# Splitting q and k into high and low parts for two attention heads in one 128-row operation, with transfers within SBUF placing each head's rows

## The chip, the cores and the metric

The kernel runs on one core of a Trainium2 chip. The metric is the device time of one execution in microseconds (us); the kernel before takes 2537.75 us, the median of 3 runs.

## What is computed

One layer of a streaming encoder on 1024 frames of width 1024: a SwiGLU block, a mixer with two branches (a gated spatial mix and stick-breaking attention), and a second SwiGLU block, with RMSNorm ahead of each and at the end. The change lies in the attention, whose reference is, cut to what matters:

```python
q, k, v = h @ W_q, h @ W_k, h @ W_v            # 16 heads of 64
z = einsum('bhtd,bhsd->bhts', q, k) / 8        # scores
log_keep = where(s < t, -softplus(z), 0)
w = where(s < t, exp(log_sigmoid(z) + reverse_cumsum(log_keep) - log_keep), 0)
y = einsum('bhts,bhsd->bhtd', w, v)
```

## The kernel before, in words

**Number format.** Products keep float32 accuracy by splitting each operand into a rounded high part and the remainder (low part), both in a format that TensorE takes at full rate. `split(hi, lo, src)` (lines 71 to 74) does it in two operations: ScalarE casts `src` to `hi` (L73), then VectorE writes `src - hi` to `lo` (L74). `mm3` (lines 65 to 69) multiplies with three matmuls.

**Projections.** `proj_t` (L76) makes 128 output columns of a projection for one half (512 frames) as a unit of 24 matmuls (8 steps of L67, L68, L69) into a PSUM bank named `pj`. In attention it takes the PSUM tag `p1`, which has 2 buffers; scores `z` have 3, transposes `tr` 2, the output `av` 1. Weights come through `load_cols`: a transfer into one of 2 `raw` buffers (L54), a cast (L56) and a subtract (L57).

**q and k of a pair.** `proj_qk(pair)` (L538) projects the 128 columns of two heads at once, q for both halves, then k for both. So a PSUM bank holds the first head in rows 0 to 63 (`lo`) and the second in rows 64 to 127 (`hi`). A score is one product over 128 rows: the tile `q[e]` has the high part in 64 rows and the low part in the other 64, `kh[e]` holds the high part of k twice, once in each half of the rows, and `kl[e]` the low part twice. Two matmuls (L572 with `kh`, L573 with `kl`) then give all four partial products. The first head (`e` = 0) has its high part of q in `lo`, the second in `hi`. Each bank takes four split operations, two for each head; the splits of q write both row halves directly, and for k four transfers on SP's queue (L556) copy 64 rows x 512 columns (128 KB) to the other row half. `q`, `kh` and `kl` have 3 buffers each, two of them taken by a pair: the first head of the next pair gets the spare one, the second head gets the one that this pair's first head gives back after its last score matmul.

**A head** (L559) goes through 8 blocks of 128 queries. Per block: scores, two sigmoids on ScalarE into `kp` (L575, 3 buffers) and `bt` (L576, 6 buffers, tag `bt`, 128x512; a block takes one `bt` or, from the fifth on, two), two masks on GpSimd (L581), a reverse cumulative product on VectorE (L583, the scan), a multiplication (L587). Then, for two blocks together, transposes on TensorE (L600), which give the `bt` buffers free, a split into `wt` (L73, L74), and the products with v (L607). The result goes through `y` (L614) to DRAM on SP's queue (L616).

**Order of the work.** The program lists the two heads of a pair, then (after every second pair) `proj_v` for the next four heads, then `proj_qk` of the next pair. The framework's scheduler, working from a simulated timeline, puts each engine's instructions and SP's transfers into one fixed order when the kernel is built; instructions listed earlier have precedence, and a tile's buffer is given out in that order too. On the chip each engine follows its order and waits for semaphores. So projections of the next pair are woven into the heads of this one. Operations of two engines on one PSUM bank are put one behind the other. The first `proj_v` alone has its TensorE order written by hand.

Of the kernel before, what the change touches and what calls it, by code (L numbers as in the profile page):

```python
# [7 lines left out]
F32 = mybir.dt.float32  # L8
F32R = mybir.dt.float32r
# [4 lines left out]
P = 128  # L14
S = 1024
# [4 lines left out]
HALF = 512  # L20
# [5 lines left out]
KPB, BTB, WTB, DVB = 3, 6, 3, 4  # L26
# [6 lines left out]
class Kernel:  # L33
# [483 lines left out]
    def attention(self, ap, ydram):  # L517
        nc, w_in = self.nc, self.a["w_in"][0]
# [17 lines left out]
            return vt  # L536

        def proj_qk(pair):  # L538
            lo, hi = slice(0, HD), slice(HD, P)
            kl = [ap.tile([P, S], F32R, tag="kl", bufs=3, name="kl") for _ in range(2)]  # L540
            q = [ap.tile([P, S], F32R, tag="q", bufs=3, name="q") for _ in range(2)]
            kh = [ap.tile([P, S], F32R, tag="kh", bufs=3, name="kh") for _ in range(2)]
            wh, wl = self.load_cols(w_in, C_Q + pair * P)
            for half in range(2):
                cs = slice(half * HALF, (half + 1) * HALF)
                ps = self.proj_t("p1", wh, wl, half)
                for e, (own, other) in enumerate(((lo, hi), (hi, lo))):
                    self.split(q[e][own, cs], q[e][other, cs], ps[own, :])
            wh, wl = self.load_cols(w_in, C_K + pair * P)
            for half in range(2):  # L550
                cs = slice(half * HALF, (half + 1) * HALF)
                ps = self.proj_t("p1", wh, wl, half)
                for e, (own, other) in enumerate(((lo, hi), (hi, lo))):
                    self.split(kh[e][own, cs], kl[e][own, cs], ps[own, :])
                    for k in (kh[e], kl[e]):
                        nc.sync.dma_start(out=k[other, cs].bitcast(F32), in_=k[own, cs].bitcast(F32))  # L556
            return [(q[e], kh[e], kl[e]) for e in range(2)]

        def head(hd, q, kh, kl, vt):  # L559
# [58 lines left out]
        with self.tc.manual_schedule(engines={mybir.EngineType.PE}):  # L618
            vts = {0: proj_v(0)}
        qk = {0: proj_qk(0)}  # L620
        npair = NHEAD // 2
        for pair in range(npair):
            for e in range(2):
                head(2 * pair + e, *qk[pair][e], vts[pair // 2])
            if pair % 2 == 1 and pair + 1 < npair:
                vts[pair // 2 + 1] = proj_v(pair // 2 + 1)
            if pair + 1 < npair:
                qk[pair + 1] = proj_qk(pair + 1)
# [249 lines left out]
```

## Time and profile before

| what | us |
|---|---|
| median of 3 runs (lowest to highest) | 2537.75 (2537.24 to 2537.94) |
| the profiled execution's own time | 2535.71 |
| its span, first to last instruction | 2534.0 |
| attention, from 715 to 1265 us of the span | 550 |
| busy in these 550 us: TensorE, VectorE, ScalarE, GpSimd | 532.75, 414.60, 326.63, 234.25 |

The mean granted clock of TensorE over the span is 0.986 of 2.4 GHz. In the profile PE is a matmul on TensorE, PEld its weight load, DVE VectorE, ACT ScalarE, POOL GpSimd and SPq the transfers that SyncE issues. A row such as `q<-pj` names the tile that is written and those that are read, without buffer numbers. `A <- B` in a list of waits means that A stood idle until B ended. Starts are in us from the start of the span.

### The profile page before, as it was taken

Reading aid. Unit: us, or ns where it says so; the run is one execution under the profiler, and the core shown is the slowest. Engines: PE = TensorE matmul, PEld = TensorE weight load, DVE = VectorE, ACT = ScalarE, POOL = GpSimd, SP = SyncE. Lnnn points to the kernel's source line nnn. Section 1 sums busy time; section 2 is a strip of 40 time slices with the busy share of each in tenths; the row PEclk is TensorE's granted clock in tenths of the full one; section 3 lists DMA queues with packets and bytes.
Section 4 is the critical chain, followed back from the end, with each engine's and each line's share of the span. In section 5 each row is a group of like instructions: output and inputs, shape, how many; then the busy total and the mean of one; then the engine's idle time right before and its main releaser. Section 6 shows DMA issues by size and latency. Waiting matters only on the chain.

```text
span 2534.0 us, 33359 instructions
## 1 busy us (share of the span) xinstructions
PE 2449.6 (97%) x12268; PEld 2074.1 (82%) x12268; DVE 1683.1 (66%) x2579; ACT 1045.2 (41%) x1996; POOL 351.7 (14%) x510
## 2 busy tenths in 40 slices
PE   6999999999999999999999999999979999999998
PEld 5788888788888888888888888888857888887886
DVE  5877787565747888786675555155838777774655
ACT  6333333344545666665422222222334333333444
POOL 4000000000214544444300000000130000000002
PEclk9999999999999999999999999999989999999999
DMA  4553553775421212122121122133445535537653
GB/s 147 175 177 124 176 178 125 292 248 183 159 57 44 67 51 76 46 72 58 39 56 53 47 88 75 58 104 125 133 125 182 174 123 176 181 127 288 235 182 133
DMA packets 257636, 326.73 MB, mean 129 GB/s; under 512 B 15680, under 2 KB 172864, under 8 KB 257472
## 3 DMA queue, kind: packets, MB, share of 16 engines
q1 hardware_dynamic: 257472, 324.60, 39.5%
q8 instruction: 96, 1.57, 0.3%
q14 instruction: 68, 0.56, 0.1%
HBM read 231.74 MB, written 84.41 MB: 125 GB/s over the span
## 4 chain that ended last, share of the span: by engine, by line
PE 85%; DVE 6%; DMA 4%; issue 2%; ACT 2%; POOL 1%; SPq 0%; POOLq 0%; ACTq 0%; DVEq 0%
PE pj L67 7%; PE pj L68 7%; PE pj L69 7%; PE pd L168 7%; PE pd L167 7%; PE pd L166 7%; PE pb L167 5%; PE pb L168 5%; PE pb L166 5%; PE av L607 3%; PE tr L600 2%; PE pv L68 2%; PE pv L69 2%; PE pv L67 2%; PE pe L167 2%
## 5 line engine op out<-in xcount | busy, mean ns | idle before, releaser
L150 ACT CAST wf<-raw 128x512 fp32r<-128x512 f32 x280 | 166.6, 620 | 244.3 <-PE pd L168 108.8
L67 PE MATMUL pj<-h,wf 128*128 128x512 f32 x640 | 254.6, 398 | 5.4 <-DVE q L74 5.4
L151 DVE TENSOR_TENSOR wf<-raw,wf 128x512 fp32r<-128x512 f32 x264 | 177.9, 695 | 119.3 <-ACT wf L150 119.0
L68 PE MATMUL pj<-h,wf 128*128 128x512 f32 x640 | 254.2, 397 | 0.0
L69 PE MATMUL pj<-h,wf 128*128 128x512 f32 x640 | 253.4, 396 | 0.0
L583 DVE TENSOR_TENSOR_SCAN kp<-kp 128x128 f32<-128x128 f32 (+7 forms) x128 | 179.7, 1412 | 37.6 <-POOL kp L581 36.1
L57 DVE TENSOR_TENSOR wf<-raw,wf 128x1024 fp32r<-128x1024 f32 x88 | 110.2, 1252 | 128.5 <-ACT wf L56 128.4
L150 ACT CAST wf<-ws 128x512 fp32r<-128x512 f32 x176 | 108.0, 622 | 190.7 <-DVE ws L159 87.4
L56 ACT CAST wf<-raw 128x1024 fp32r<-128x1024 f32 x88 | 92.7, 1053 | 214.4 <-PE pj L68 117.9
L587 POOL TENSOR_TENSOR bt<-bt,kp 128x512 f32<-128x512 f32 (+4 forms) x128 | 130.3, 1021 | 130.5 <-DVE kp L583 98.0
L67 PEld LDWEIGHTS pj<-h,wf 128*128 128x128 f32 x640 | 122.3, 191 | 31.0 <-DVE q L74 6.8
L67 PE MATMUL pv<-wf,h 128*128 128x256 f32 x512 | 145.2, 286 | 2.5 <-ACT vg L650 2.1
L68 PE MATMUL pv<-wf,h 128*128 128x256 f32 x512 | 145.7, 285 | 0.3 <-DVE wf L57 0.3
L69 PE MATMUL pv<-wf,h 128*128 128x256 f32 x512 | 145.2, 284 | 0.0
L69 PEld LDWEIGHTS pj<-h,wf 128*128 128x128 f32 x640 | 122.0, 191 | 24.6 <-DVE wf L57 0.2
L68 PEld LDWEIGHTS pj<-h,wf 128*128 128x128 f32 x640 | 122.1, 191 | 24.0
L114 POOL TENSOR_TENSOR xn<-x,gain 128x512 f32<-128x512 f32 x12 | 16.7, 1391 | 893.2 <-DVE x L474 601.7
L166 PE MATMUL pb<-T,wf 128*128 128x512 f32 x352 | 137.4, 390 | 0.0
L167 PE MATMUL pb<-T,wf 128*128 128x512 f32 x352 | 137.2, 390 | 0.0
L168 PE MATMUL pb<-T,wf 128*128 128x512 f32 x352 | 136.8, 389 | 0.0
L167 PE MATMUL pd<-wf 128*128 128x512 f32 x344 | 134.7, 392 | 0.2 <-DVE wf L151 0.2
L166 PE MATMUL pd<-wf 128*128 128x512 f32 x344 | 132.8, 393 | 1.9 <-DVE x L463 1.4
(216 smaller groups left out, 6589.3 us busy)
## 6 DMA issues: line engine op xcount, KB each, us to landing
raw<-in_ff_w_down_dram SPq DMA_DIRECT2D x66, 512.0 KB, 6.2
raw<-in_w_in_dram SPq DMA_DIRECT2D x56, 512.0 KB, 3.8
raw<-in_ff_w_gate_dram SPq DMA_DIRECT2D x52, 512.0 KB, 4.3
raw<-in_ff_w_up_dram SPq DMA_DIRECT2D x44, 512.0 KB, 5.5
f_t2t<-as SPq DMA_DIRECT2D x22, 512.0 KB, 4.9
f_a11a<-act SPq DMA_DIRECT2D x44, 256.0 KB, 4.1
f_s2s<-as SPq DMA_DIRECT2D x22, 512.0 KB, 2.9
f_s3s<-as SPq DMA_DIRECT2D x22, 512.0 KB, 5.6
```

The costliest lines, as they stand in the source:

```text
L56: nc.scalar.copy(hi, raw)
L57: (nc.gpsimd if early else nc.vector).tensor_tensor(lo, raw, hi.bitcast(F32), op=ALU.subtract)
L67: mm(ps, lhsT=lh, rhs=rh, start=first, stop=False)
L68: mm(ps, lhsT=lh, rhs=rl, start=False, stop=False)
L69: mm(ps, lhsT=ll, rhs=rh, start=False, stop=last)
L150: self.nc.scalar.copy(f[:, 0, :], src)
L151: (sub or self.nc.vector.tensor_tensor)(f[:, 1, :], src, f[:, 0, :].bitcast(F32), op=ALU.subtract)
L166: mm(ps, lhsT=lh, rhs=rh, start=first, stop=False, skip_group_check=True)
L167: mm(ps, lhsT=lh, rhs=rl, start=False, stop=False, skip_group_check=True)
L168: mm(ps, lhsT=ll, rhs=rh, start=False, stop=last, skip_group_check=True)
L583: nc.vector.tensor_tensor_scan(rev, rev, rev, 1.0, op0=ALU.mult, op1=ALU.bypass)
L587: eng.tensor_tensor(bt[:, :n], bt[:, :n], kp[:, i * HALF + 1:i * HALF + 1 + n], op=ALU.mult)
```

## The change

One split over all 128 rows of a bank replaces the two of 64 rows. For q the high parts of both heads go to the tile of the second head, where the second head's are in their place; the low parts go to a new tile `qlo`, which takes one of the 6 `bt` buffers. Three transfers per half then put the first head's high part, the first head's low part and the second head's low part where they belong; the last overwrites the rows of the second head's tile out of which the first has copied. For k both parts of both heads go to the second head's tiles, and three transfers for each of `kh` and `kl` copy the first head's rows to both row halves of its own tiles, and then the second head's rows over the first's. Per pair there are 4 casts and 4 subtracts of 128x512 where there were 8 and 8 of 64x512, and 18 transfers of 128 KB where there were 8. There are 8 pairs.

```diff
             wh, wl = self.load_cols(w_in, C_Q + pair * P)
             for half in range(2):
                 cs = slice(half * HALF, (half + 1) * HALF)
-                ps = self.proj_t("p1", wh, wl, half)
-                for e, (own, other) in enumerate(((lo, hi), (hi, lo))):
-                    self.split(q[e][own, cs], q[e][other, cs], ps[own, :])
+                qlo = ap.tile([P, HALF], F32R, tag="bt", bufs=BTB, name="qlo")
+                self.split(q[1][:, cs], qlo, self.proj_t("p1", wh, wl, half))
+                move(q[0][lo, cs], q[1][lo, cs])
+                move(q[0][hi, cs], qlo[lo, :])
+                move(q[1][lo, cs], qlo[hi, :])
             wh, wl = self.load_cols(w_in, C_K + pair * P)
             for half in range(2):
                 cs = slice(half * HALF, (half + 1) * HALF)
-                ps = self.proj_t("p1", wh, wl, half)
-                for e, (own, other) in enumerate(((lo, hi), (hi, lo))):
-                    self.split(kh[e][own, cs], kl[e][own, cs], ps[own, :])
-                    for k in (kh[e], kl[e]):
-                        nc.sync.dma_start(out=k[other, cs].bitcast(F32), in_=k[own, cs].bitcast(F32))
+                self.split(kh[1][:, cs], kl[1][:, cs], self.proj_t("p1", wh, wl, half))
+                for k in (kh, kl):
+                    for rows in (lo, hi):
+                        move(k[0][rows, cs], k[1][lo, cs])
+                    move(k[1][lo, cs], k[1][hi, cs])
```

`move(dst, src)` is a transfer on SP's queue, as before. The order in which the three sets of tiles are listed is unchanged.

## Rows read from the trace of the kernel before

**Rows 1.** The page, part 1: busy us (share of the span) and instructions of an engine.

```profile
PE 2449.6 (97%) x12268; PEld 2074.1 (82%) x12268; DVE 1683.1 (66%) x2579; ACT 1045.2 (41%) x1996; POOL 351.7 (14%) x510
```

**Rows 2.** Windows: length, busy PE, PEld, DVE, ACT, POOL, granted clock, DMA share, GB/s.

```profile
755.00:775.00 20.00, 14.99 (x69) 12.13 (x69) 15.28 (x19) 9.45 (x22) 9.67 (x14) 0.83 0.15 41
...
775.00:885.00 110.00, 109.37 (x732) 100.06 (x731) 89.87 (x103) 72.53 (x159) 52.15 (x85) 1.00 0.25 61
...
885.00:895.00 10.00, 6.52 (x30) 5.53 (x29) 9.69 (x12) 6.26 (x15) 5.08 (x10) 0.83 0.26 82
...
1005.00:1025.00 20.00, 16.06 (x78) 12.97 (x76) 15.65 (x16) 11.46 (x26) 8.25 (x15) 0.83 0.19 47
...
1135.00:1155.00 20.00, 16.95 (x82) 13.88 (x82) 15.48 (x18) 11.57 (x27) 9.41 (x17) 0.83 0.16 41
```

**Rows 3.** Waits of PE, 715 to 1270 us: us in total, times, longest.

```profile
PE tr L600 <- DVE wt L74: 6.2, 3, 3.3
...
PE pj L67 <- DVE q L74: 5.4, 4, 3.1
```

**Rows 4.** Timeline, first place: start, us, engine, line, operation [idle before <-releaser].

```profile
754.73 0.40 PE L573 MATMUL z<-kl,q 128*128 128x512 f32 x1
...
755.25 0.58 ACT L73 CAST q<-pj 64x512 fp32r<-64x512 f32 x1
...
757.58 0.58 ACT L73 CAST q<-pj 64x512 fp32r<-64x512 f32 x1
...
757.69 0.68 DVE L74 TENSOR_TENSOR q<-pj,q 64x512 fp32r<-64x512 f32 x1
...
758.40 4.21 DVE L583 TENSOR_TENSOR_SCAN kp<-kp 128x896 f32<-128x896 f32 x2
...
762.64 0.69 DVE L74 TENSOR_TENSOR q<-pj,q 64x512 fp32r<-64x512 f32 x1
...
763.39 0.79 PE L67 MATMUL pj<-h,wf 128*128 128x512 f32 x1 [3.07 <-DVE q L74]
```

**Rows 5.** Timeline, fourth place.

```profile
1136.50 0.39 PE L573 MATMUL z<-kl,q 128*128 128x512 f32 x1
...
1136.52 0.68 DVE L74 TENSOR_TENSOR q<-pj,q 64x512 fp32r<-64x512 f32 x1
...
1138.37 1.06 ACT L73 CAST q<-pj 64x512 fp32r<-64x512 f32 x2
...
1141.34 1.30 DVE L74 TENSOR_TENSOR q<-pj,q 64x512 fp32r<-64x512 f32 x2
...
1142.09 0.80 PE L67 MATMUL pj<-h,wf 128*128 128x512 f32 x1 [1.09 <-DVE q L74]
```

**Rows 6.** Groups by line and form, 715 to 1270 us: busy us, mean ns, idle before.

```profile
L74 DVE TENSOR_TENSOR q<-pj,q 64x512 fp32r<-64x512 f32 x32 | 21.8, 688 | 10.4 <-ACT q L73 9.8
...
L74 DVE TENSOR_TENSOR wt<-tr,wt 128x512 fp32r<-128x512 f32 x96 | 64.5, 680 | 26.5 <-ACT wt L73 26.0
...
L73 ACT CAST q<-pj 64x512 fp32r<-64x512 f32 x32 | 18.5, 583 | 21.1 <-DVE q L74 10.5 <-PE pj L69 10.4
...
L73 ACT CAST wt<-tr 128x512 fp32r<-128x512 f32 x96 | 56.8, 597 | 42.3 <-PE tr L600 42.0
```

**Rows 7.** Timeline, second place, PE.

```profile
892.39 0.50 PE L67 MATMUL pj<-h,wf 128*128 128x512 f32 x1 [0.23 <-DVE q L74]
```

**Rows 8.** Waits of ACT, 715 to 1270 us: us in total, times, longest.

```profile
ACT bt L576 <- PE tr L600: 15.0, 19, 2.9
```

**Rows 9.** The tile kh, and timelines of SP and PE, odd-to-even hand-over.

```profile
L556 SPq DMA_DIRECT2D kh<-kh x32: 461/476/570, 733.4 to 1165.4; - x32
...
DMA to landing us min/median/max: 2.2/2.3/4.4
...
859.78 0.48 SPq L556 DMA_DIRECT2D kl<-kl  x1
...
863.82 0.28 PE L573 MATMUL z<-kl,q 128*128 128x128 f32 x1
```

More of the change, by code (lines that the diff above doesn't have):

```diff
@@ L539, in proj_qk, with move @@
             lo, hi = slice(0, HD), slice(HD, P)
-            kl = [ap.tile([P, S], F32R, tag="kl", bufs=3, name="kl") for _ in range(2)]
-            q = [ap.tile([P, S], F32R, tag="q", bufs=3, name="q") for _ in range(2)]
-            kh = [ap.tile([P, S], F32R, tag="kh", bufs=3, name="kh") for _ in range(2)]
+            kl, q, kh = ([ap.tile([P, S], F32R, tag=tag, bufs=3, name=tag) for _ in range(2)] for tag in ("kl", "q", "kh"))
+            def move(dst, src):
+                nc.sync.dma_start(out=dst.bitcast(F32), in_=src.bitcast(F32))
             wh, wl = self.load_cols(w_in, C_Q + pair * P)
```

## The prediction, made before the changed kernel ran

> **What bounds the kernel now.** I read the views from coarse to fine. The busy table shows TensorE busy for 97% of the span and VectorE for 66% [rows 1], so a VectorE or ScalarE instruction that goes pays only where TensorE stands still for it. The stages by windows say where that is: of the whole attention, TensorE idles in four places. In the first it is busy for 15.0 of 20.0 us, in the second for 6.5 of 10.0, in the third for 16.1 of 20.0, in the fourth for 17.0 of 20.0; the idle sums to 15.5 us (5.0, 3.5, 3.9, 3.1), the granted clock there is 0.83 and VectorE is up to 97% busy, while the 110 us between the first two have 0.6 us idle at clock 1.00 [rows 2]. A mean clock of 0.83 between levels of 1.2 and 2.4 GHz costs 0.17 of the 70 us, 11.9 us more. So 27.4 us is all that this change can find there; elsewhere TensorE is full.
>
> These four places are the hand-overs from an even pair to the next (0 to 1, 2 to 3, ...), where no v projection lies between. The waits name what TensorE stands for: the subtract of a weight split (6.2 us) and the subtract of q (5.4 us) [rows 3]. The q wait is a PSUM one. The first K unit needs the bank of the first q unit, which is free when both heads' splits have read it; the second head's tile is the one that the pair's first head still reads as q. In the timeline that head's last score matmul starts at 754.73; the second head's cast follows at 757.58, its subtract only at 762.64, because one q subtract (757.69) and two scans (4.21 us) stand before it on VectorE; TensorE goes on at 763.39 after 3.07 us [rows 4]. The fourth place shows it again: last score matmul 1136.50, casts from 1138.37, subtracts from 1141.34, TensorE at 1142.09 after 1.09 us [rows 5].
>
> **The change, part by part.** *Splits.* Per pair 8 casts and 8 subtracts on 64 rows become 4 and 4 on 128 rows. A subtract of 64 rows takes 688 ns, one of 128 rows and as many columns 680; a cast 583 against 597 [rows 6]. So 32 subtracts (22 us of VectorE) and 32 casts (18 us of ScalarE) go, at no price per row. For the odd-to-even hand-overs, and for all K splits, the cover is a full TensorE [rows 2], and I count nothing there. If that cover failed, each late subtract would cost its 0.7 us.
>
> *The four places.* The single q split writes the second head's tile, so it too waits for the last score matmul; nothing comes earlier for that reason. What goes is the first head's own split. At the first place a q subtract stands ahead of the scans [rows 4]; its cast ran at 755.25, after that last score matmul, so the combined split can have that slot, and the bank is free about 5 us sooner. TensorE's wait for it was 3.07 us: I take -3.1. At the second place the order is the same, but TensorE reached the matmul late and waited 0.23 us [rows 7]: -0.2. At the third and fourth place the early subtract (1136.52) has a cast from before the last score matmul [rows 5], so its slot is no use; the combined one keeps its place behind the scan, and only the 0.68 us ahead of it goes: -0.7 each, below the 1.09 us that TensorE waited. Sum -4.7 us. Below this lies nothing (the freed time is taken up by the next scan), above it the whole 15.5 us. *Clock*: idle at the first place falls from 5.0 to 1.9 us. 3.1 us of idle went with 0.83 and 0.6 us with 1.00 [rows 2]; 1.9 lies between, so I take half of that place's 3.4 us: -1.7, between 0 and -11.9.
>
> *The bt slots.* The low part of q gets one of the six bt buffers per half (16 in all) from its subtract until two transfers have landed. Six are not plenty: ScalarE waited 19 times, 15.0 us in all, at most 2.9 us, for transposes to free one [rows 8]. Behind the waiting q subtract stand scans and weight splits on VectorE. Bounds per place: 0 and +2.9 us. I take 0, since at the first place head 1's scores have barely begun when the slot is wanted, and a bt is then free as soon as one weight block is transposed.
>
> *Transfers.* 8 per pair become 18: 80 more, each about 0.48 us of SP's queue [rows 9]. They land in 2.3 us (median) [rows 9]. What is behind them on SP are weight loads and y stores; they have their buffers' time to spare while TensorE is full, so 0. q's low rows now come by transfer as well, but a K unit ahead of need. The second head's low rows of k are overwritten after both copies out of them have landed, one landing (2.3 us) and one issue later than the first head's; that head starts half a pair later. For the first head the danger is order: at an odd-to-even hand-over its kl transfer is issued at 859.78 and the score matmul that reads it runs at 863.82 [rows 9], 1.7 us after 859.78 + 2.3. Bounds 0 and +2.0 us per hand-over (below), taken 0: nothing obliges kl to wait for the second head's k.
>
> The Trainium skill speaks against such transfers ("SBUF — State Buffer", section "Can I just issue two DMAs to hit both halves?" and the table above it): rows 0 to 63 reach 8 of 16 ports, and two transfers on the two halves hardly overlap. At its rate for 8 ports two 128 KB moves one behind the other would land about 0.6 us apart (an estimate from that page). The trace shows no such spread: the 64-row moves, issued about 0.7 us apart, land in 2.2 to 4.4 us with a median of 2.3 [rows 9], and no run so far has three of them in flight. With the page's spread the fourth rival below would be 0.6 us dearer per hand-over.
>
> *Sum.* -4.7 - 1.7 = -6.4 us on the profiled execution's 2535.7 us (span 2534.0): 2529.3. That execution is 2.0 us under the median of the runs, 2537.75, which gives **2531.3 us**. About 0.2% (5.1 us) is what a measurement can tell from no change.
>
> **The rivals.** *Deeper.* The stall goes at all four places and the clock stays up at some: -15.5 - 3 = 2519. For it: VectorE is the only engine full there. Against: TensorE has only scores, transposes and the K unit to do, and the heads' share hangs on the same scans. Chance 0.10.
>
> *Taken up elsewhere.* The K unit that starts sooner at the first place is then missing as filler some 10 us later, so that 3.1 us comes back and the clock falls all the same; the 0.7s at two places and 0.2 remain: -1.6, 2536. For it: the weight subtract's 6.2 us of waits [rows 3] stay. Chance 0.27.
>
> *The slot (slower).* The q subtract waits for a bt slot at each of the four places, with VectorE's queue behind it: the longest wait of its kind, 2.9 us [rows 8], less the 0.7 saved, four times: +8.8 us, 2546.5. It decides from a wait of 2.0 us per place on (then +5.2). For it: the slots must carry the four blocks of the old head's last rows and the new head's first two just then. Chance 0.17.
>
> *Transfers late (slower).* If SP issues the overwrite of the second head's kh before the first head's kl, kl waits for a landing and three issues, 2.3 + 3 x 0.48 = 3.7 us, 2.0 beyond the 1.7 of slack, at four hand-overs: +8.0, 2545.8. Against: the order is chosen from what is ready. Chance 0.08.
>
> **How the numbers follow.** The forecast has 0.38; faster is 0.38 + 0.10 = 0.48, same 0.27, slower 0.17 + 0.08 = 0.25. The range goes from the deeper case, 2519, to the slot case, 2547; with half of each rival's chance at its end beyond these, under 2 in 10 is outside. The forecast's own range is 2527 to 2533.
>
> **What would show it.** In the profile after: q and kh casts and subtracts 16 each, 128 x 512, near 597 and 680 ns; 144 transfers instead of 64, landing near 2.3 us. Right: the first of the four windows with 2 us idle and a clock above 0.9, the q wait of TensorE near 1 us in all, VectorE 22 us less. The slot rival: a q subtract waiting for a transpose. The transfer rival: score matmuls waiting for a DMA. The forecast is wrong if TensorE's idle in attention stays at its sum, or if idle appears outside the four places, where I counted every part as hidden.

## The result, and the profile after

The changed kernel takes 2563.82 us (median of 4 runs, 2562.61 to 2564.68) where the kernel before takes 2537.49 on the same chip (2536.06 to 2537.94): a ratio of 1.0105 with a 95% interval of 1.0092 to 1.0118. It is 26.3 us slower where 6.4 us less were forecast, and the time lies outside the range. The profiled execution has a span of 2563.0 us, 29.0 more than before, at a mean granted clock of 0.983 (0.986 before).

The busy row of the page answers to [rows 1].

```profile
PE 2467.9 (96%) x12268; PEld 2083.8 (81%) x12268; DVE 1655.8 (65%) x2547; ACT 1028.4 (40%) x1964; POOL 352.4 (14%) x510
```

VectorE has 32 instructions and 27.3 us less, ScalarE 32 and 16.8 us less. So the change does what it says, and the time was lost in another place. The groups by line and form, over attention (715 to 1295 us), answer to [rows 6]: 16 of each instead of 32, at almost the durations that the rows of before gave.

```profile
L74 DVE TENSOR_TENSOR kl<-pj,kh 128x512 fp32r<-128x512 f32 x16 | 11.0, 688 | 18.4 <-ACT kh L73 18.4
...
L74 DVE TENSOR_TENSOR qlo<-pj,q 128x512 fp32r<-128x512 f32 x16 | 10.7, 676 | 3.6 <-ACT q L73 3.6
...
L73 ACT CAST q<-pj 128x512 fp32r<-128x512 f32 x16 | 9.5, 595 | 12.9 <-PE pj L69 12.9
```

The windows answer to [rows 2] (length, busy PE, PEld, DVE, ACT, POOL, granted clock, DMA share, GB/s). The first four are the even-to-odd hand-overs, now 40 us long each, the last two the stages behind attention.

```profile
755.00:795.00 40.00, 29.91 (x161) 24.84 (x161) 34.23 (x36) 22.45 (x50) 19.08 (x31) 0.87 0.23 53
885.00:925.00 40.00, 32.26 (x178) 26.67 (x177) 35.45 (x37) 26.24 (x59) 25.79 (x37) 0.91 0.22 50
1025.00:1065.00 40.00, 33.79 (x174) 28.66 (x174) 33.83 (x38) 23.25 (x52) 22.20 (x31) 0.83 0.27 61
1155.00:1195.00 40.00, 31.86 (x174) 26.32 (x173) 35.35 (x38) 25.33 (x56) 23.14 (x34) 0.91 0.23 53
1285.00:1700.00 415.00, 414.77 (x2262) 360.22 (x2261) 212.74 (x420) 104.63 (x175) 17.79 (x32) 1.00 0.22 67
1700.00:2563.00 863.00, 827.52 (x3626) 678.82 (x3624) 571.47 (x902) 316.78 (x568) 49.22 (x44) 0.98 0.49 164
```

The idle of TensorE in the four is 10.09 + 7.74 + 6.21 + 8.14 = 32.2 us, and the clock costs at most (0.13 + 0.09 + 0.17 + 0.09) x 40 = 19.2 us (if TensorE is busy all the time at the lower clock): 51.4 in all, where the prediction counted 15.5 + 11.9 = 27.4 before in the same way. Its windows are shorter, but they held nearly all the idle there was: 15.5 of the 17.3 us that TensorE was idle from 715 to 1265 us. Counted so, these four places got 24.0 us dearer, most of the 29.0. By time of day: attention's last copy to `y` comes 18.8 us later than before (1284.2 against 1265.4). The last 863 us of the two executions hold the same work (3626 and 3630 matmuls on record); the stretch between is 415 us instead of 406, as the same view of the kernel before shows.

```profile
1265.00:1671.00 406.00, 403.11 (x2209) 350.08 (x2209) 210.55 (x419) 103.33 (x174) 18.17 (x32) 1.00 0.22 67
1671.00:2534.00 863.00, 827.33 (x3630) 679.37 (x3628) 572.76 (x902) 317.61 (x569) 48.93 (x44) 0.98 0.49 164
```

TensorE is full in that stretch in both kernels; after the change it has 53 matmuls more there (2262 against 2209 on record) and 11.7 us more of busy time. These ran within attention before: 3265 matmuls are on record from 715 to 1265 us there, 3215 from 715 to 1285 us after the change.

What happens at the first place is in its timeline (start, us, engine, line, operation); it answers to [rows 4].

```profile
744.42 0.59 ACT L73 CAST q<-pj 128x512 fp32r<-128x512 f32 x1 [1.31 <-PE pj L69]
...
752.23 0.58 ACT L73 CAST q<-pj 128x512 fp32r<-128x512 f32 x1
...
755.71 0.40 PE L579 MATMUL z<-kl,q 128*128 128x512 f32 x1
...
756.14 1.11 SPq L545 DMA_DIRECT2D q<-q  x2
...
785.47 2.27 DVE L589 TENSOR_TENSOR_SCAN kp<-kp 128x1024 f32<-128x1024 f32 x1
...
785.89 0.63 ACT L582 ACTIVATE bt<-z 128x512 f32<-128x512 f32 x1
...
787.67 1.26 DVE L74 TENSOR_TENSOR qlo<-pj,q 128x512 fp32r<-128x512 f32 x2
...
788.38 0.50 PE L67 MATMUL pj<-h,wf 128*128 128x512 f32 x1 [1.64 <-DVE qlo L74]
```

The two casts run at 744.42 and 752.23, the first 11 us before the current pair's first head has its last score matmul (755.71). Their subtracts run one behind the other from 787.67 on: 43 and 36 us behind the casts, and right behind the last `bt` of the pair's second head (785.89). Until then both `p1` banks hold q units that are only half read, so the first K unit, TensorE's filler, starts at 788.38 instead of 763.39. The other three places are alike: casts at 881.64, 1015.09 and 1149.29, first subtracts at 921.07, 1055.26 and 1189.11, each between the second head's last two `bt` writes (920.59 and 921.54 at the second place); the K units start at 921.9, 1056.1 and 1190.0, where before they started at 892.4, 1015.9 and 1142.1. At the odd-to-even hand-overs nothing is late: no subtract starts more than 1.3 us behind the start of its cast (at the first, casts at 854.01 and 862.48, subtracts at 854.63 and 863.75).

The waits hardly show this (us in total, times, longest; PE and ACT, 715 to 1295 us; they answer to [rows 3] and [rows 8]).

```profile
PE av L613 <- DVE wt L74: 25.4, 24, 2.9
PE z L578 <- ACT bt L582: 2.4, 8, 0.4
PE pj L67 <- DVE qlo L74: 1.6, 1, 1.6
...
ACT bt L582 <- PE tr L606: 10.8, 13, 2.7
```

TensorE waits 1.6 us for `qlo` and 25.4 us for weight splits: without filler it runs at the pace of the heads' own chain of scans and splits. The waits of `bt`, by which the prediction priced the slots, even fell, from 15.0 to 10.8 us. The order of VectorE was fixed when the kernel was built, with other work ahead of the late subtract, so its lateness stands in no list as a wait for a buffer: it shows in how far the subtract stands from its cast.

The transfers are as forecast: the moves out of `qlo` are 32 in number (with 48 each for `kh` and `kl`, and 16 of q's high part, 144), and land as those of [rows 9] did (the tile `qlo`):

```profile
L545 SPq DMA_DIRECT2D q<-qlo x32: 461/477/602, 723.2 to 1193.1; - x32
...
DMA to landing us min/median/max: 2.2/2.3/4.4
```

### The profile page after: what moved, and what is told of

Its sections match the earlier page's. It is cut to its first block, busy times and chain, and to the rows that moved or that the text cites. A ratio compares the mean times of both kernels' runs of the same rounds, so it can differ in the third digit from the quotient of the medians.

```text
span 2563.0 us, 33368 instructions
## 1 busy us (share of the span) xinstructions
PE 2467.9 (96%) x12268; PEld 2083.8 (81%) x12268; DVE 1655.8 (65%) x2547; ACT 1028.4 (40%) x1964; POOL 352.4 (14%) x510
## 4 chain that ended last, share of the span: by engine, by line
PE 58%; DVE 5%; DMA 2%; issue 2%; POOL 1%; ACT 1%; SPq 0%; POOLq 0%; ACTq 0%; DVEq 0%
PE pj L67 6%; PE pj L68 6%; PE pj L69 6%; PE pd L168 3%; PE pd L167 3%; PE pd L166 3%; PE pb L167 2%; PE pb L168 2%; PE pb L166 2%; PE av L613 2%; PE pv L69 2%; PE pv L67 2%; PE pv L68 2%; PE tr L606 2%; DVE kp L589 1%
## 5 line engine op out<-in xcount | busy, mean ns | idle before, releaser
L67 PE MATMUL pj<-h,wf 128*128 128x512 f32 x640 | 250.6, 392 | 1.6 <-DVE qlo L74 1.6
L68 PE MATMUL pj<-h,wf 128*128 128x512 f32 x640 | 250.5, 391 | 0.0
L69 PE MATMUL pj<-h,wf 128*128 128x512 f32 x640 | 250.4, 392 | 0.0
L593 POOL TENSOR_TENSOR bt<-bt,kp 128x512 f32<-128x512 f32 (+4 forms) x128 | 137.2, 1074 | 110.9 <-DVE kp L589 95.3
L613 PE MATMUL av<-wt,v 128*128 128x256 f32 (+1 forms) x640 | 120.1, 299 | 26.2 <-DVE wt L74 25.4
L67 PEld LDWEIGHTS pj<-h,wf 128*128 128x128 f32 x640 | 120.3, 188 | 25.1 <-DVE qlo L74 1.8
L69 PEld LDWEIGHTS pj<-h,wf 128*128 128x128 f32 x640 | 120.2, 188 | 24.0 <-DVE wf L57 0.4
L68 PEld LDWEIGHTS pj<-h,wf 128*128 128x128 f32 x640 | 120.3, 188 | 23.2
L167 PE MATMUL pd<-wf 128*128 128x512 f32 x344 | 134.8, 392 | 0.0
```

The source lines that it names most:

```text
L67: mm(ps, lhsT=lh, rhs=rh, start=first, stop=False)
L68: mm(ps, lhsT=lh, rhs=rl, start=False, stop=False)
L69: mm(ps, lhsT=ll, rhs=rh, start=False, stop=last)
L167: mm(ps, lhsT=lh, rhs=rl, start=False, stop=False, skip_group_check=True)
L593: eng.tensor_tensor(bt[:, :n], bt[:, :n], kp[:, i * HALF + 1:i * HALF + 1 + n], op=ALU.mult)
L613: nc.tensor.matmul(av[:, ac + o0:ac + 256], lhsT=lhs, rhs=wt[:, part, jj * 256:jj * 256 + 256 - o0], start=j0 + jj + part == 0, stop=diag ...
```

## The experiments

The theory: `qlo` shares the tag `bt`, whose buffers are given out in listing order, and it is listed behind all blocks of the pair's second head; so its subtract gets a buffer only when that head has been given its last `bt`. The rivals: six buffers are too few; the transfers delay the work; the operations on 128 rows or the k part cost something. All ratios are to the kernel before, on the same chip, with a 95% interval; the edits are to the changed kernel except in the last.

**A buffer of its own for `qlo`.**

```diff
-                qlo = ap.tile([P, HALF], F32R, tag="bt", bufs=BTB, name="qlo")
+                qlo = ap.tile([P, HALF], F32R, tag="qlo", bufs=1, name="qlo")
```

> The changed kernel, but the low part of q gets one buffer of its own instead of one of the six bt buffers. Theory (buffer precedence): the subtract of q is late only because a bt buffer is given to it after every block of the odd head, which is listed earlier, has had its own. Then with its own buffer the subtracts at the four even-to-odd hand-overs stand within 12 us of their casts (37 to 43 us in the changed kernel), TensorE's idle in the stretch from 715 to 1285 us falls from 34 us to 16 us or less, and the time is 2525 to 2538 us. Rival (transfers): the 80 more transfers on SP and the hand-over through them hold the heads up; the time stays at 2555 us or more. Rival (fewer bt for the heads): the heads lack a buffer while q holds it; this kernel gives it back, so it also predicts a fall here, but tells itself apart in the run with seven bt buffers.

Measured: 2508.71 us against 2536.66, ratio 0.9886 (0.9869 to 0.9902). This beats both kernels. In its timeline the first half's subtract follows its cast at once, and the first K unit starts at 750.47.

```profile
743.58 0.59 ACT L73 CAST q<-pj 128x512 fp32r<-128x512 f32 x1 [1.31 <-PE pj L69]
...
744.33 0.66 DVE L74 TENSOR_TENSOR qlo<-pj,q 128x512 fp32r<-128x512 f32 x1
...
750.47 0.39 PE L67 MATMUL pj<-h,wf 128*128 128x512 f32 x1
...
751.39 0.58 ACT L73 CAST q<-pj 128x512 fp32r<-128x512 f32 x1
...
761.03 0.39 PE L579 MATMUL z<-kl,q 128*128 128x512 f32 x1
...
761.92 0.55 SPq L545 DMA_DIRECT2D q<-q  x1
...
767.63 0.68 DVE L74 TENSOR_TENSOR qlo<-pj,q 128x512 fp32r<-128x512 f32 x1
```

The second half's subtract comes 16 us behind its cast, since there is one buffer and the first half's transfers still hold it; at the other three places it is 8 to 13 us. Those transfers wait too: they write the first head's q tile, whose buffer the current pair's first head gives back after its last score matmul (761.03), and they are issued from 761.92 on. So part of the old wait is still there, but it holds `qlo` and the second bank instead of both banks. One free bank is enough: TensorE has its filler, and the windows of the four places show 0.7, 0.0, 1.1 and 0.0 us of idle at clock 1.00.

```profile
745.00:775.00 30.00, 29.28 (x173) 25.55 (x172) 24.86 (x26) 19.27 (x41) 18.75 (x25) 1.00 0.39 89
865.00:895.00 30.00, 30.00 (x184) 26.54 (x183) 25.57 (x28) 19.86 (x44) 17.31 (x28) 1.00 0.39 89
985.00:1015.00 30.00, 28.89 (x169) 25.05 (x168) 24.22 (x26) 17.76 (x38) 16.02 (x25) 1.00 0.33 82
1105.00:1135.00 30.00, 30.00 (x168) 25.82 (x167) 26.08 (x27) 17.25 (x37) 13.56 (x24) 1.00 0.42 95
```

So with a buffer of its own for one tile the loss of 26 us is a gain of 28. The expected time, 2525 us or more, was too high, as I had not counted on all four stalls going.

**Seven `bt` buffers, still shared** (`BTB` from 6 to 7).

> The changed kernel with seven bt buffers instead of six, q's low part still among them. Theory (buffer precedence): a seventh buffer goes to the odd head as well, the q subtract still comes after its last block, 30 us or more after its cast, and the time stays within 10 us of the changed kernel's 2564. Rival (fewer bt for the heads): the number was short by one, the time falls to 2540 us or less, as with a buffer of its own. Rival (transfers): 2560 or more.

Measured: 2580.97, ratio 1.0177 (1.0162 to 1.0192): slower still, and not within the 10 us of the changed kernel that were expected. The rival of the transfers (2560 or more) holds as a number, but the run before has the same transfers and takes 2508.71. Its timeline has the second head's last `bt` at 783.29 and the subtract behind it; at the second place the subtracts wait for a transpose.

```profile
783.29 0.62 ACT L582 ACTIVATE bt<-z 128x512 f32<-128x512 f32 x1
...
785.13 0.67 DVE L74 TENSOR_TENSOR qlo<-pj,q 128x512 fp32r<-128x512 f32 x1
...
923.76 1.29 DVE L74 TENSOR_TENSOR qlo<-pj,q 128x512 fp32r<-128x512 f32 x2 [1.27 <-PE tr L606]
```

Capacity is not the cause: with a buffer more, which is the memory of the run before, the subtracts still come 33 to 43 us behind their casts, and the kernel is 72 us slower than that run. TensorE's idle at the four places (745 to 785, 885 to 925, 1025 to 1065 and 1165 to 1205 us) is 42.4 us, 10 more than with six; why it grows no run settles.

**The k part alone** (q as before) and **the q part alone** (k as before). The diff is that of k alone, cut.

```diff
-                self.split(q[1][:, cs], qlo, self.proj_t("p1", wh, wl, half))
-                move(q[0][lo, cs], q[1][lo, cs])
...
+                for e, (own, other) in enumerate(((lo, hi), (hi, lo))):
+                    self.split(q[e][own, cs], q[e][other, cs], ps[own, :])
```

> Only k's part of the change: k split in 128 rows and placed by twelve transfers per pair, q as in the kernel before, no low tile of q in bt. Theory (buffer precedence): nothing of the loss is in k; 2528 to 2540 us. Rival (transfers): 64 of the 80 extra transfers less the q ones, that is 32 more than before, and the order of the copies are still there; 2548 us or more.

> Only q's part of the change: q split in 128 rows with its low part in a bt buffer and six transfers per pair, k as in the kernel before. Theory (buffer precedence): the whole loss is here; 2555 to 2568 us, and the q subtracts at the four hand-overs 30 us or more after their casts. Rival (transfers): less than half of the loss, 2550 us or less.

Measured: k alone 2534.03, ratio 0.9994 (0.9984 to 1.0003), no change; q alone 2575.59, ratio 1.0155 (1.0140 to 1.0170), above the 2568 that were expected at most. The loss is all in q; with q's subtracts late (785.78 at the first place), the k part takes something back, as 1.0155 becomes 1.0105 with it.

**Own buffer and five `bt`**, which together take the memory of the changed kernel.

> The low part of q in one buffer of its own and only five bt buffers for the heads: the same memory as the changed kernel's six. Theory (buffer precedence): whose turn it is decides, not how many there are; the q subtracts come within 20 us of their casts, TensorE keeps its filler and the time is 2505 to 2530 us. Rival (fewer bt for the heads): with one bt less all the time it is as slow as the changed kernel or slower, 2555 us or more.

Measured: 2527.54, ratio 0.9970 (0.9959 to 0.9982). So a gain is to be had in the memory of the change, but a sixth `bt` beside the own buffer is worth most of it (2508.71). ScalarE's waits for a `bt` don't show this price. They are 39.1 us in this run, but 39.0 with the own buffer and six `bt`, against the 15.0 of [rows 8]; the two lines are of this run and of that one.

```profile
ACT bt L582 <- PE tr L606: 39.1, 28, 5.3
...
ACT bt L582 <- PE tr L606: 39.0, 31, 4.8
```

What differs is the second half's subtract: at three places it comes 28 to 37 us behind its cast, not within the 20 that were expected, and TensorE idles 12.3 us from 715 us to the end of attention (1255), where the own buffer with six leaves 2.1 us (to 1237). At the second place:

```profile
862.84 0.58 ACT L73 CAST q<-pj 128x512 fp32r<-128x512 f32 x1
...
891.13 0.67 DVE L74 TENSOR_TENSOR qlo<-pj,q 128x512 fp32r<-128x512 f32 x1
```

**Own buffer, q part alone; and own buffer, with each split cut in two of 64 rows**, which has as many operations as the kernel before, but all transfers of the change. The diff is q's part of the latter.

```diff
-                self.split(q[1][:, cs], qlo, self.proj_t("p1", wh, wl, half))
+                ps = self.proj_t("p1", wh, wl, half)
+                for rows in (lo, hi):
+                    self.split(q[1][rows, cs], qlo[rows, :], ps[rows, :])
```

> The low part of q in one buffer of its own, q split in 128 rows, k split in 64 rows for each head as before. Theory (bank set free early): the gain of 28 us over the kernel before comes from the q banks, which no longer wait for the pair's first head; 2507 to 2517 us. Rival (fewer operations): half of the 22 us of VectorE saved are k's, so about half of the gain goes; 2518 to 2530 us.

> As with the buffer of its own, same tiles and transfers, but each split done as two of 64 rows, so as many casts and subtracts as before the change (32 + 32 more than with the buffer of its own). Theory (bank set free early): what counts is that the bank is read into a tile which is free; most of the gain stays, 2508 to 2520 us. Rival (fewer operations): the gain is in the number of casts and subtracts; 2528 us or more.

Measured: 2517.04, ratio 0.9932 (0.9917 to 0.9947), and 2519.77, ratio 0.9942 (0.9927 to 0.9957), both against 2535.76. With no operation saved, 16.0 us are gained all the same. That is the part of the tile: the one written first gets the spare q buffer, so the q splits need not wait for this pair's first head. The other 12 of the 27.9 us (27.9 - 16.0) come with the halved operations, 9 of them with those of k (27.9 - 18.7), which alone had changed nothing. What is left to the halved operations of q, 2.7 us, is within the two intervals, and the first of the two times lies at the border of what theory and rival had given (2517 and 2518); the second decides for the theory.

**The shared tag, with a higher precedence.**

```diff
-                qlo = ap.tile([P, HALF], F32R, tag="bt", bufs=BTB, name="qlo")
-                self.split(q[1][:, cs], qlo, self.proj_t("p1", wh, wl, half))
+                ps = self.proj_t("p1", wh, wl, half)
+                with self.tc.high_priority():
+                    qlo = ap.tile([P, HALF], F32R, tag="bt", bufs=BTB, name="qlo")
+                    self.split(q[1][:, cs], qlo, ps)
```

> The changed kernel with its six shared bt buffers, but the framework is told to give the q split (its buffer, cast and subtract) precedence over what is listed before it. Theory (buffer precedence): the subtract comes within 20 us of its cast and the time falls to 2540 us or less, with nothing else changed. Rival (fewer bt for the heads): precedence takes a buffer from the heads at their tightest point, so it stays at 2555 us or more.

Measured: 2563.85, ratio 1.0116 (1.0101 to 1.0132): a miss of the theory, which gave 2540 or less. The rival's 2555 or more holds as a number; its mechanism needs an early subtract, and there is none. The subtracts still stand behind the second head's last `bt`.

```profile
784.51 0.63 ACT L584 ACTIVATE bt<-z 128x512 f32<-128x512 f32 x1
...
786.29 1.25 DVE L74 TENSOR_TENSOR qlo<-pj,q 128x512 fp32r<-128x512 f32 x2
```

Precedence, set in this way, did not change the turn for a buffer.

**The shared tag, with q of the next pair listed ahead of this pair's second head** (`proj_qk` cut into a q and a k part).

```diff
             for e in range(2):
+                if e == 1 and pair + 1 < npair:
+                    nxt = proj_q(pair + 1)
                 head(2 * pair + e, *qk[pair][e], vts[pair // 2])
```

> The changed kernel, six shared bt buffers, with the q part of the next pair's projection listed ahead of the pair's second head instead of behind it; k's part stays where it was. Theory (buffers go by the order of the listing, whatever the precedence): the q subtracts no longer come behind the odd head's last block; they stand within 15 us of their casts, the stalls at the even-to-odd hand-overs go, and the time is 2540 us or less although the heads share six buffers with q. Rival (fewer bt for the heads): the two low tiles now hold up the odd head's first blocks instead; 2555 us or more.

Measured: 2570.38, ratio 1.0132 (1.0113 to 1.0150). The subtracts moved with the listing: now they follow the first head's last `bt` and stand ahead of the second head's first, which waits for their transfers.

```profile
763.64 0.61 ACT L590 ACTIVATE bt<-z 128x512 f32<-128x512 f32 x1
...
767.97 1.26 DVE L74 TENSOR_TENSOR qlo<-pj,q 128x512 fp32r<-128x512 f32 x2
...
772.32 0.28 ACT L590 ACTIVATE bt<-z 128x128 f32<-128x128 f32 x1 [2.96 <-DMA q<-qlo]
```

The place in the list thus sets the turn. But the time did not fall to the 2540 or less of the theory; it is in the band of the rival (2555 or more), by which the low tiles now hold up the second head's first blocks. The subtracts are still 16 to 23 us behind their casts (744.72 and 752.53), they are now late at the odd-to-even hand-overs too (casts 797.76 and 804.41, subtracts from 824.28 on), and the heads pay too, in a wait of ScalarE that the kernel before does not have:

```profile
ACT bt L590 <- DMA q<-qlo: 16.9, 11, 3.0
```

In both places of the list `qlo` waits for a head, and in this one a head waits for it too.

**The kernel before, with a spare q buffer for both heads**, and the memory taken from `y`.

```diff
-            q = [ap.tile([P, S], F32R, tag="q", bufs=3, name="q") for _ in range(2)]
+            q = [ap.tile([P, S], F32R, tag="q", bufs=4, name="q") for _ in range(2)]
...
-                    y = ap.tile([P, HALF], F32, tag="y", bufs=2, name="y")
+                    y = ap.tile([P, HALF], F32, tag="y", bufs=1, name="y")
```

> The kernel before, with a fourth q buffer (and one y buffer instead of two, for room), so that the second head's split need not wait for the first head's last score. Theory (bank set free early): that wait was what held the q banks at the four places, and most of the gain that the buffer of its own gave comes without the change: 2512 to 2527 us. Rival (fewer operations): it is VectorE's load that makes the four places; 2530 us or more.

Measured: 2515.91 (2512.28 to 2525.29) against 2535.24, ratio 0.9933 (0.9910 to 0.9957). The K units now follow the q units at once, so the hand-overs come earlier than in [rows 2]; the windows around the four q units and what follows them:

```profile
740.00:770.00 30.00, 30.00 (x168) 26.05 (x167) 26.37 (x29) 19.46 (x42) 16.20 (x26) 1.00 0.32 80
850.00:880.00 30.00, 30.00 (x168) 25.99 (x167) 25.00 (x28) 18.66 (x40) 16.39 (x23) 1.00 0.28 69
970.00:1000.00 30.00, 30.00 (x166) 25.95 (x165) 24.11 (x28) 18.96 (x41) 16.59 (x23) 1.00 0.27 68
1090.00:1125.00 35.00, 35.00 (x200) 30.48 (x199) 28.93 (x33) 21.21 (x46) 18.36 (x25) 1.00 0.26 64
```

No idle is left at these places, without any part of the change; in the whole of attention (715 to 1241 us) TensorE idles 5.6 us where it was 17.3. So the stalls before were indeed the wait for the second head's tile, and a free tile is what the own-buffer versions have in common with this one.

## Why the prediction was wrong

**What bounds the kernel: right.** Most of what was won or lost lies at the four places, with q's PSUM banks (24.0 of the 29.0 us). The bound of 27.4 us on what can be found there was met: the own buffer brought 27.9, and its four windows hold 1.8 us of idle.

**Splits: right.** 32 subtracts and 32 casts went, at 676 to 688 and 595 ns for 128 rows where 680 and 597 were taken. What they are worth depends on the banks: nothing for k alone, about 12 us once the banks come free early.

**"The single q split writes the second head's tile, so it too waits for the last score matmul; nothing comes earlier": wrong.** That tile is now the one written first, and it got the spare buffer, while the first head's tile got the one that is given back: the casts run up to 11 us before that score matmul (755.71), and the first transfers into the first head's tile are issued right behind it, at 756.14. This hid the gain of 16 us that the run with 64-row splits shows, and the -4.7 and -1.7 us of the forecast, sized on the old order, answer to nothing.

**The bt slots, taken as 0 with a bound of +2.9 us per place: the step that failed.** The account of the kernel before says itself that a tile's buffer is given out in listing order; the step did not apply that to `qlo`. (What counts is where a tile's first write is listed: of q's two tiles the one created second is written first and was served first.) It argued that a `bt` is free as soon as a block is transposed. It is, but the next turn belongs to the second head's next block, and so on to its last: the subtracts came 33 to 43 us after their casts at the four places. The bound was no bound, because [rows 8] are waits of instructions whose turn it was. What the step put at 0 measures some 54 us: the loss of 26.3 here and the gain of 28 that the same change brings with a buffer of its own. The slot rival had the right resource and sign but this same price, and so gave +8.8 us where 26.3 were measured. The sign it looked for, a q subtract waiting for a transpose, is absent from the trace of the changed kernel; VectorE did other work in its fixed order.

**Transfers, taken as 0: right.** The k part alone has 32 transfers more than the kernel before and the same time. The own buffer with 64-row splits has 80 more than the last experiment, and their ratios, 0.9942 and 0.9933, lie within each other's intervals. The Trainium skill ("SBUF — State Buffer", section "Can I just issue two DMAs to hit both halves?") says that transfers on the two halves serialize; no run here shows a price for it, and the median landing stayed at 2.3 us. One reading of the prediction is wrong here: transfers of this kind had been in flight three at a time before, as those issued at 733.38, 734.06 and 734.67 us of the kernel before, where none lands in less than 2.2 us.

**The other rivals.** *Deeper* (all four stalls go) is what the own buffer reaches, and exceeds: 2508.71 against the 2519 it was given. *Taken up elsewhere* has the time of k alone (2534.03), where a saving came to nothing; whether by its mechanism is not shown. *Transfers late* fell: TensorE's waits for the transfers of `kl` are 0.3 us in all.

**What stays open.** Why seven shared buffers are slower than six; why the k part helps by half a per cent when q is late or early, and not with the q of before; and the 5.0 us of the longer span that the four places don't hold, of which 2.6 are there because the two profiled executions lie off their medians. The own buffer's second half still waits 8 to 16 us; two own buffers were not tried.

## What to carry to other kernels

A short-lived tile that borrows a buffer from a rotating tag took its turn in listing order here, and a higher precedence did not change that: count which tiles of that tag are listed ahead of it and when the last of them is served, and don't price it by the waits that the tag shows today. Then ask what it holds meanwhile: here a PSUM bank, and with it the filler of the bounding engine. When a change adds a tile, one buffer of its own is the first thing to compare with; and when it changes which tile is written first, see which buffer that tile now gets.

## What the runs showed that was not expected

A loss of 26 us appears as 1.6 us in the list of waits for the tile that caused it; the distance between a cast and its subtract shows it, the waits don't. Where TensorE lacked filler the granted clock, of 2.4 GHz, was 0.83 to 0.91 over stretches of 40 us, and 1.00 at the same hand-overs with the own buffer, so that of the 24.0 us which those places lost, by the same count, 7.3 (19.2 - 11.9) are clock and not idle time.
